# When finished sums are taken out of PSUM: gating traced at each job's end, and fill work kept back behind a chain step

## The chip, the cores and the metric

The kernel runs on one core of one Trainium2 chip. The metric is the device time of one execution in microseconds. Each version is timed in several runs and the median is given. One further execution runs under the hardware profiler, and all durations inside the kernel come from it.

## The reference

One inference step of a hybrid encoder layer for 512 new frames of one stream and 64 frames of a running one, 576 in all, with 2048 channels:

```
h = RMSNorm(x);  z = h @ w_in
y_a = rwkv7(r, k, v, decay, alpha of z) * silu(g_a)
y_b = windowed_attention(q, k, v of z) * silu(g_b)
merged = sigmoid(m_a) * (y_a @ p_a) + sigmoid(m_b) * (y_b @ p_b)
y = RMSNorm(x + merged @ w_o)
```

`rwkv7` carries a 64x64 state per head through time; with 16 heads, each frame updates the state by a decay, a rank-one correction and a new key-value product, and reads it with r. Everything is fp32. The states, the shifted row and the key and value caches are outputs too.

## The kernel before

**Layout.** Channels lie on the 128 partitions and the 576 frames on the free axis. A large product is split in two halves of 256 and 320 frames, one PSUM bank each (`ga`, `gb`). For precision each weight and each input is a pair of a high and a low part, and a product is three matmuls per half (high by high, high by low, low by high).

**Jobs.** A `Job` makes one block of 128 output channels. Its `step()` (line 131) issues the six matmuls of one of its 16 or 8 blocks of input channels. Jobs stand in the list `jobs`, and `pump(n)` issues the next n steps of whichever job is first. `need(job)` (line 158) steps until that job is over and returns its result. When the last step is traced, `done` is called with the two PSUM halves and traces what takes them out: for most jobs `scaled` (line 206), two VectorE products with the RMSNorm factor, which is line 208 in the profile. Weights come in quarters of a job of 16 steps (four steps, `QK`): `prefetch` (line 104) issues the DMA of a quarter (`wr`), ScalarE's copy to its high part (`wh`, line 118) and VectorE's subtraction for the low part (`wl`, line 119), so that up to four quarters are in `ready`. It is called whenever a quarter has been used up, and its work has the planner's high priority.

**Order.** Only TensorE's order is written out by hand: its instructions run in the order in which they are traced. For the other engines a planner chooses the order from dependences and priorities; instructions traced earlier come first where both are ready. Each engine then runs its own queue in order. A block under `tc.issue_after(i)` puts its instructions on i's engine behind i.

**The chain.** The recurrent part handles the heads in eight pairs. In each pair, `rwkv` (line 549) goes through nine chunks of 64 frames in eight steps (the last step has two chunks). A step is a chain: VectorE forms the state `SV` and its scaled form `s0p` (lines 686 to 690), TensorE multiplies them (`p0`, lines 691 and 692), VectorE copies the result to `r0` (line 694), TensorE multiplies by the solved triangle `XT` (line 698), VectorE negates that into `UV` (lines 701 and 702), TensorE forms the next state `sp` and the outputs `py` (lines 707 to 716). While VectorE works, TensorE is filled with steps of jobs: `pump(PUMP["c1"])` behind r0's trace, `pump(PUMP["c2"])` behind UV's, both under `issue_after`, and `pump(PUMP["c3"])` (line 721) behind the outputs, under nothing. Each is one step, with one more in the first c1 of a pair. A job has 16 steps and a pair's chain 25 fills, so a job or a quarter ends now in one kind of fill, now in another.

**The output projections.** Behind the recurrent part come 16 blocks of merged output (lines 793 to 821). For block j there is a job on `p_b` and one on `p_a`, eight steps each, created in the order p_b(j), p_b(j+1), p_a(j), p_a(j+1) for even j. Their `done` returns the PSUM halves as they are. The loop over j takes them out: `gated` (line 793) multiplies the halves with a sigmoid tile `sg` loaded from DRAM (line 801), first `mb` with p_b's result, then `ma` with p_a's; their sum is split into a high and a low part for the last projection. `need` of p_a(j) runs p_b(j+1) and p_a(j), so the gating of p_b(j+1) is traced behind that of p_a(j). Each of the tags `ga` and `gb` has two PSUM buffers.

Of the kernel before, what the change touches and what calls it, by code (L numbers as in the profile page):

```python
# [18 lines left out]
NA = 256  # L19
NB = NT - NA  # L20
# [25 lines left out]
def tile_layer(ctx: ExitStack, tc: tile.TileContext, A: dict):  # L46
# [45 lines left out]
        return hi, lo  # L92

    plan, ready, jobs, spare = deque(), {}, deque(), deque()
    QK = 4

    def halfpass(w, x, out, kk, sl, first, last):
# [6 lines left out]
    def prefetch():  # L104
        while len(ready) < 4 and (plan or spare):
            if not plan:
                spare.popleft()()
                continue
            job, q = plan.popleft()
            with tc.high_priority() if len(h) == KT and jobs[0].own is None else nullcontext():  # L110
                src = wp.tile([P, QK, P], F32, tag="wr", name="wr", bufs=WR)
                nc.sync.dma_start(src.rearrange("p k c -> p (k c)"), job.w[q // 2][:, (q % 2) * QK * P : (q % 2 + 1) * QK * P])
                ready[job, q] = wsplit(src, wp, 4)
# [8 lines left out]
    class Job:  # L122
# [8 lines left out]
        def step(self):  # L131
            k = self.k
            if k == 0 and self.banks:
                self.pa, self.pb = self.banks
            elif k == 0:
                self.pa = pg.tile([P, 512], F32, tag="ga", name="ga")
                self.pb = pg.tile([P, 512], F32, tag="gb", name="gb")
            hi, lo = self.own[k // QK] if self.own else ready[self, k // QK]
            xh, xl = self.xs[k]
            for w, x, f, e in ((hi, xh, k == 0, False), (hi, xl, False, False), (lo, xh, False, k == self.nk - 1)):  # L140
                nc.tensor.matmul(self.pa[:, :NA], w[:, k % QK, :], x[:, 0:NA], start=f, stop=e)  # L141
                nc.tensor.matmul(self.pb[:, :NB], w[:, k % QK, :], x[:, NA:NT], start=f, stop=e)  # L142
            self.k += 1
            if self.k % QK == 0 and not self.own:
                del ready[self, k // QK]
                prefetch()
            if self.k == self.nk:
                jobs.remove(self)
                self.over = True
                self.result = self.done((self.pa[:, :NA], self.pb[:, :NB]))  # L150

    def pump(n):
        for _ in range(n):
# [4 lines left out]
    def need(job):  # L158
        while not job.over:
            jobs[0].step()  # L160
        return job.result

    def mm2(*terms):
# [385 lines left out]
    def rwkv(p, r, k, v, kk, Pd, Qd, b, gate, ahead, before):  # L549
# [48 lines left out]
        for j in range(UB - 1):  # L598
            n, m = UB - 1 - j, j // SP + 1
# [74 lines left out]
        for cs in (*((c,) for c in range(7)), (7, 8)):  # L674
            g = cs[0] // 3
            T, NM, XT, TK = Ts[g], NMs[g], XTs[g], TKs[g]
            at = [(n * L, c, c - 3 * g) for n, c in enumerate(cs)]
            w = len(cs) * L
            if cs[0] == 3 * g:
                py = pst()  # L680
            s0p = r2.tile([P, 2 * L], F32, tag="s0p", name="s0p")
            p0 = pst()
            for n, c, i in at:
                if c not in (0, 8):
                    sp, pt, prev = S_prev
                    dve.scalar_tensor_tensor(SV[E, c, 0:64], sp[E, 0:64], pt[E], prev[E, 0:64], op0=ALU.mult, op1=ALU.add)  # L686
                    dve.scalar_tensor_tensor(SV[O, c, 64:128], sp[O, 0:64], pt[O], prev[O, 0:64], op0=ALU.mult, op1=ALU.add)
                pt = PT[:, c : c + 1]
                dve.tensor_scalar(s0p[E, n : n + L], SV[E, c, 0:64], pt[E], None, op0=ALU.mult)
                dve.tensor_scalar(s0p[O, n : n + L], SV[O, c, 64:128], pt[O], None, op0=ALU.mult)  # L690
                nc.tensor.matmul(p0[E, n : n + L], T[:, i, 0, 0:64], SV[:, c, 0:64], start=True, stop=True)  # L691
                nc.tensor.matmul(p0[O, n : n + L], T[:, i, 1, 0:64], SV[:, c, 64:128], start=True, stop=True)
            r0 = r2.tile([P, 2 * L], F32, tag="r0", name="r0")
            with tc.issue_after(dve.tensor_copy(r0[:, 0:w], p0[:, 0:w]).ins):  # L694
                pump(PUMP["c1"] + (cs[0] == 0) * PUMP["c0"])
            pu = pst()
            for n, c, i in at:
                nc.tensor.matmul(pu[:, n : n + L], XT[:, i, :], r0[:, n : n + L], start=True, stop=True)  # L698
            ui = slice(cs[0], cs[-1] + 1)
            pu3 = pu[:, 0:w].rearrange("p (i c) -> p i c", c=L)  # L700
            dve.tensor_scalar(UV[E, ui, 0:64], pu3[E], -1.0, None, op0=ALU.mult)  # L701
            tip.append(dve.tensor_scalar(UV[O, ui, 64:128], pu3[O], -1.0, None, op0=ALU.mult).ins)
            with tc.issue_after(tip[-1]):
                pump(PUMP["c2"])
            sp = pst()
            for n, c, i in at:
                nc.tensor.matmul(sp[E, n : n + L], TK[:, i, 0:64], UV[:, c, 0:64], start=True, stop=True)  # L707
                nc.tensor.matmul(sp[O, n : n + L], TK[:, i, 64:128], UV[:, c, 64:128], start=True, stop=True)  # L708
            S_prev = (sp, pt, s0p)
            for n, c, i in at:  # L710
                for u, h_ in ((0, E), (1, O)):
                    hc = slice(64 * u, 64 * u + 64)
                    nc.tensor.matmul(py[h_, i * 64 : (i + 1) * 64], SV[:, c, hc], T[:, i, u, 64:128], start=True, stop=False)
                for u, h_ in ((0, E), (1, O)):
                    hc = slice(64 * u, 64 * u + 64)
                    nc.tensor.matmul(py[h_, i * 64 : (i + 1) * 64], UV[:, c, hc], NM[:, i, 128 + 64 * u : 192 + 64 * u], start=False, stop=True)  # L716
                if c >= 7:
                    so = r2.tile([P, L], F32, tag="so", name="so")
                    dve.scalar_tensor_tensor(so, sp[:, n : n + L], PT[:, c : c + 1], s0p[:, n : n + L], op0=ALU.mult, op1=ALU.add)
                    nc.sync.dma_start(A["wkv"][c - 7, p], so)  # L720
            pump(PUMP["c3"])
            if cs[-1] == 3 * g + 2:
                q = slice(g * 192, (g + 1) * 192)
                act(ysb[0][:, q], py[:, 0:192], AF.Copy)  # L724
                yr = r2.tile([P, 192], F32, tag="NU", name="yr", bufs=1)
                act(yr, py[:, 0:192], AF.Copy)  # L726
                pool.tensor_tensor(ysb[1][:, q], yr, ysb[0][:, q].bitcast(F32), op=ALU.subtract)  # L727
# [51 lines left out]
    with ExitStack() as ph:  # L779
        yp = {n: ph.enter_context(tc.tile_pool(name=n, bufs=16)) for n in ("yap", "ybp")}  # L780
        t2 = ph.enter_context(tc.tile_pool(name="t2", bufs=5))
        ys = []
        for n, src in (("ybp", yb_d), ("yap", ya_d)):
            l_ = []
            for k in range(8):
                raw = t2.tile([P, NT], F32, tag="t", name="yraw")
                nc.gpsimd.dma_start(raw, src[k])
                l_.append(split(raw, yp[n], "y", f"y{k}"))
            ys.append(l_)
        while jobs or spare:  # L790
            pump(1)

        def gated(sg, psum, name):
            o = t2.tile([P, NT], F32, tag="t", name=name)
            for (x, y), z in zip(halves(), psum):
                dve.tensor_tensor(o[:, x:y], sg[:, x:y], z, op=ALU.mult)
            return o

        def load_sg(i):
            s = t2.tile([P, NT], F32, tag="sg", name="sg", bufs=6)  # L800
            nc.sync.dma_start(s, sg_d[i])
            return s

        pj = [[None, None] for j in range(KT)]
        for j in range(0, KT, 2):
            for i, n in enumerate(("p_b", "p_a")):
                for d in range(2):
                    pj[j + d][i] = Job([A[n][j + d]], ys[i], lambda psum: psum)
        mg = [None] * KT
        wo = []  # L810
        sg = [[load_sg(2 * j), load_sg(2 * j + 1)] for j in range(2)]
        for j in range(KT):
            if j + 2 < KT:
                sg.append([load_sg(2 * j + 4), load_sg(2 * j + 5)])
            if j == KT - 2:
                wo = [Job(A["w_o"][m], mg, lambda psum: psum) for m in range(KT - DEFER)]
            mb = gated(sg[j][1], need(pj[j][0]), "mb")
            ma = gated(sg[j][0], need(pj[j][1]), "ma")
            dve.tensor_tensor(ma, ma, mb, op=ALU.add)
            mg[j] = split(ma, hp, "hh", f"mg{j}")  # L820

    with ExitStack() as ph:
# [42 lines left out]
        for m in range(KT - DEFER):  # L865
            psum = need(wo[m])
# [123 lines left out]
```

## Time and profile before

| | |
|---|---|
| runs before | 1788.28, 1788.43, 1789.96 us; median 1788.43 us |
| profiled execution | 1788.85 us, of which the span from first to last instruction is 1787.1 us |
| granted TensorE clock, mean over the span | 0.996 |
| HBM traffic | 104 GB/s over the span |

A profile row gives an engine, a source line, the tiles written and read, a count, a time, and often in brackets the idle time of the engine before it and what ended that. "L119 DVE wl" is VectorE's subtraction of line 119. "PE" is TensorE's matmuls, "PEld" its weight loads, ACT is ScalarE, POOL is GpSimd, SP the queue that issues DMAs. In the timeline, rows begin with the start in us from the start of the span and the duration. The chain of work is followed back from the last instruction: each row is a piece of it with its start and length.

### The profile page before, as it was taken

How to read it: one execution, taken by the hardware profiler on the slowest of the kernel's cores; microseconds unless marked ns; L12 is line 12 of the kernel's file. 1: busy time of each engine (PE TensorE's matmuls, PEld its weight loads, DVE VectorE, ACT ScalarE, POOL GpSimd, SP SyncE). 2: the span in 40 equal slices, each digit the busy share in tenths (PEclk: the TensorE clock that was granted, in tenths of full speed). 3: DMA queues.
4: the chain of work that ended last, by engine and by line, in shares of the span. 5: the costliest groups of instructions: out<-in, count | busy, mean ns of one | idle time of the engine just before them, and what ended most of it. 6: DMA issues, size and time to landing. Idle time of an engine off the chain costs nothing.

```text
span 1787.1 us, 36090 instructions
## 1 busy us (share of the span) xinstructions
PE 1752.9 (98%) x14393; PEld 1695.5 (95%) x14393; DVE 1101.6 (62%) x2479; ACT 694.6 (39%) x1308; POOL 336.9 (19%) x448
## 2 busy tenths in 40 slices
PE   9999999999999999999999999999999999999996
PEld 8999999999989999899898998989999999999996
DVE  7445445567777678687786877768655434342224
ACT  7455546543333434244332443424234222243321
POOL 0112212242111312214222241222020000001112
PEclk9999999999999999999999999999999999999998
DMA  7322222333324233233232332323346333253323
GB/s 230 118 87 76 87 87 73 96 96 100 120 82 114 84 98 107 68 113 97 88 110 75 107 95 83 115 72 104 114 137 211 125 123 124 93 168 103 110 73 107
DMA packets 158601, 190.92 MB, mean 107 GB/s; under 512 B 52640, under 2 KB 81600, under 8 KB 158432
## 3 DMA queue, kind: packets, MB, share of 16 engines
q1 hardware_dynamic: 157152, 183.89, 32.9%
q0 software_dynamic: 1280, 4.72, 0.7%
q8 instruction: 113, 1.85, 0.4%
q14 instruction: 56, 0.46, 0.1%
HBM read 158.42 MB, written 27.03 MB: 104 GB/s over the span
## 4 chain that ended last, share of the span: by engine, by line
PE 88%; DVE 7%; DMA 2%; issue 1%; ACT 1%; POOL 1%; DVEq 0%; SPq 0%; ACTq 0%; POOLq 0%
PE gb L142 40%; PE ga L141 34%; DVE wl L119 1%; PE s L707 1%; PE s L691 1%; PE s L698 1%; PE s L142 1%; PE s L168 1%; DVE sg L208 1%; DVE o L861 1%; PE s L141 1%; PE s L305 1%; DVE T L563 1%; DVE T L562 1%; PE s L304 1%
## 5 line engine op out<-in xcount | busy, mean ns | idle before, releaser
L118 ACT ACTIVATE wh<-wr 128x512 fp32r<-128x512 f32 x460 | 288.9, 629 | 719.0 <-PE gb L142 634.4
L119 DVE TENSOR_TENSOR wl<-wr,wh 128x512 fp32r<-128x512 f32 x460 | 333.7, 729 | 267.1 <-ACT wh L118 263.5
L847 POOL TENSOR_TENSOR sq<-sq 128x256 f32<-128x256 f32 (+1 forms) x28 | 25.4, 925 | 378.1 <-ACT sq L841 378.0
L602 DVE TENSOR_TENSOR tmp<-NU,XU 108x84 f32<-108x84 f32 (+23 forms) x248 | 64.2, 259 | 14.3 <-DMA NU<-n_d 8.5
L604 DVE TENSOR_TENSOR XU<-XU,tmp 108x84 f32<-108x84 f32 (+23 forms) x248 | 68.5, 276 | 6.1
L727 POOL TENSOR_TENSOR ylo<-yr,yhi 128x192 fp32r<-128x192 f32 x24 | 14.7, 612 | 298.2 <-ACT yr L726 251.7
L219 POOL COPY praw<-praw 128x7 f32<-128x7 f32 x25 | 9.2, 368 | 218.5 <-DVE praw L216 218.4
L701 DVE TENSOR_SCALAR UV<-s 64x64 f32<-64x64 f32 x64 | 14.4, 224 | 47.6 <-PE s L698 47.6
L329 ACT ACTIVATE sc<-sc,nm 128x256 f32<-128x256 f32 (+2 forms) x80 | 37.1, 466 | 13.6 <-DVE nm L327 13.5
L384 ACT ACTIVATE sg<-sg 128x576 f32<-128x576 f32 x32 | 21.9, 684 | 49.1 <-DVE sg L208 49.0
L235 POOL TENSOR_TENSOR gateb<-gateb,z 128x576 f32<-128x576 f32 x8 | 11.4, 1420 | 150.3 <-ACT gateb L234 150.3
L334 POOL TENSOR_TENSOR sc<-sc,es 128x768 f32<-128x768 f32 x16 | 27.6, 1723 | 63.7 <-ACT wh L118 58.0
L565 POOL TENSOR_TENSOR BK<-k,Qd 64x192 f32<-64x192 f32 x48 | 34.0, 707 | 27.0 <-DVE k L544 21.3
L222 POOL TENSOR_TENSOR d<-praw 128x576 f32<-128x576 f32 x25 | 35.5, 1421 | 0.0
L564 POOL TENSOR_TENSOR BK<-b,Qd 64x192 f32<-64x192 f32 x48 | 32.6, 680 | 11.3 <-PE s L583 8.4
L686 DVE SCALAR_TENSOR_TENSOR SV<-s,PT,s0p 64x64 f32<-64x64 f32 x56 | 15.4, 276 | 27.4 <-PE s L708 27.0
L223 DVE SCALAR_TENSOR_TENSOR d<-d,vec,praw 128x576 f32<-128x576 f32 x25 | 22.2, 890 | 15.8 <-POOL d L222 15.8
L742 DVE RECIPROCAL sd<-sd 128x576 f32<-128x576 f32 x8 | 30.0, 3753 | 3.1 <-ACT sd L741 3.0
L540 DVE RECIPROCAL nrm<-nrm 128x576 f32<-128x576 f32 x8 | 30.0, 3750 | 1.1 <-ACT nrm L539 1.1
L698 PEld LDWEIGHTS s<-r,XT 128*128 128x128 f32 x144 | 22.9, 190 | 6.7 <-DVE r L694 6.7
L698 PE MATMUL s<-r,XT 128*128 128x64 f32 x144 | 23.8, 256 | 4.8 <-DVE r L694 4.8
L724 ACT ACTIVATE yhi<-s 128x192 fp32r<-128x192 f32 x24 | 8.0, 332 | 52.5 <-PE s L716 51.9
(1147 smaller groups left out, 7248.9 us busy)
## 6 DMA issues: line engine op xcount, KB each, us to landing
wr<-in_w_in SPq DMA_DIRECT2D x340, 256.0 KB
wr<-in_w_o SPq DMA_DIRECT2D x56, 256.0 KB
sg_d<-sg SPq DMA_DIRECT2D x32, 288.0 KB
sg<-sg_d SPq DMA_DIRECT2D x32, 288.0 KB
wr<-in_p_b SPq DMA_DIRECT2D x32, 256.0 KB
wr<-in_p_a SPq DMA_DIRECT2D x32, 256.0 KB
x<-in_xT SPq DMA_DIRECT2D x16, 288.0 KB
n_d<-nm SPq DMA_DIRECT2D x24, 192.0 KB
```

The source lines that it names most:

```text
L118: act(hi, src, AF.Copy)
L119: dve.tensor_tensor(lo, src, hi.bitcast(F32), op=ALU.subtract)
L141: nc.tensor.matmul(self.pa[:, :NA], w[:, k % QK, :], x[:, 0:NA], start=f, stop=e)
L142: nc.tensor.matmul(self.pb[:, :NB], w[:, k % QK, :], x[:, NA:NT], start=f, stop=e)
L222: pool.tensor_tensor(d, p[:, :, 0:64], p[:, :, 1:65], op=ALU.subtract)
L329: act(sc[:, a:b], sc[:, a:b], AF.Exp, bias=nm[:, i : i + 1], accum_out=dn[:, i : i + 1])
L540: dve.reciprocal(nrm, nrm)
L564: pool.tensor_tensor(BK[h_, :, 64 * u : 64 * u + 64], b[h_, cs_, :], Qd[h_, cs_, :], op=ALU.mult)
L565: pool.tensor_tensor(BK[h_, :, 64 - 64 * u : 128 - 64 * u], k[h_, cs_, :], Qd[h_, cs_, :], op=ALU.mult)
L602: dve.tensor_tensor(t_, NU[:, j, j + 1 : UB].unsqueeze(1).to_broadcast([SP * UN, m, n]), XU[:, 0:m, j : j + 1].to_broadcast([SP * UN, m, n ...
L604: dve.tensor_tensor(XU[:, 0:m, j + 1 : UB], XU[:, 0:m, j + 1 : UB], t_, op=ALU.add)
L698: nc.tensor.matmul(pu[:, n : n + L], XT[:, i, :], r0[:, n : n + L], start=True, stop=True)
```

## The change

A function `later(f)` runs f at once, or puts it in a queue while the list `holding` is not empty; `flush()` runs what is queued. `step` hands `prefetch` and the job's `done` (now in a method `end`) to `later`. `holding` is filled only around the c3 fill of a chain step. The queue is run behind the next chain step's r0 copy, inside its `issue_after`; at the end of `need`; where a weight quarter is wanted that isn't loaded yet; and at once behind the last chain step. So the scaled copies and the weight quarter that a c3 fill triggers are traced one half step later. TensorE's order stays as it was.

In the output projections, `done` of each job now does the gating itself, so that `mb` and `ma` are traced at the end of the job that they belong to.

```
+    held, holding = deque(), []
+
+    def later(f):
+        if holding:
+            held.append(f)
+        else:
+            f()
+
+    def flush():
+        while held:
+            held.popleft()()
...
+            if not self.own and (self, k // QK) not in ready:
+                flush()
...
                 del ready[self, k // QK]
-                prefetch()
+                later(prefetch)
             if self.k == self.nk:
                 jobs.remove(self)
                 self.over = True
-                self.result = self.done((self.pa[:, :NA], self.pb[:, :NB]))
+                later(self.end)
+
+        def end(self):
+            self.result = self.done((self.pa[:, :NA], self.pb[:, :NB]))
...
         while not job.over:
             jobs[0].step()
+        flush()
         return job.result
...
             with tc.issue_after(dve.tensor_copy(r0[:, 0:w], p0[:, 0:w]).ins):
+                flush()
                 pump(PUMP["c1"] + (cs[0] == 0) * PUMP["c0"])
...
+            holding.append(cs)
             pump(PUMP["c3"])
+            holding.pop()
+            if cs[-1] == 8:
+                flush()
...
-                    pj[j + d][i] = Job([A[n][j + d]], ys[i], lambda psum: psum)
+                    pj[j + d][i] = Job([A[n][j + d]], ys[i], lambda psum, i=i, j=j + d: gated(sg[j][1 - i], psum, "ma" if i else "mb"))
...
-            mb = gated(sg[j][1], need(pj[j][0]), "mb")
-            ma = gated(sg[j][0], need(pj[j][1]), "ma")
+            mb, ma = [need(i) for i in pj[j]]
```

## The prediction

> **What bounds the kernel now.** I read the page's first part, then the waits of PE, then the chain of work that ended last, and then single stretches of the timeline.
>
> ```profile
> span 1787.1 us, 36090 instructions
> PE 1752.9 (98%) x14393; PEld 1695.5 (95%) x14393; DVE 1101.6 (62%) x2479; ACT 694.6 (39%) x1308; POOL 336.9 (19%) x448
> ```
>
> TensorE is busy for 98% of the span, so the kernel is bound by PE nearly everywhere, and a change that adds and removes no instruction can only win what PE spends waiting: the span less PE's busy time, 1787.1 - 1752.9 = 34.2 us, at most. The waits of PE (engine, line, releaser; then total us, times, longest) begin with the two that matter here:
>
> ```profile
> PE s L698 <- DVE r L694: 4.8, 7, 0.7
> PE ga L141 <- ACT wh L118: 4.1, 9, 0.5
> ```
>
> The first belongs to the chain step (L694 is the copy r0, L698 the product behind it), seven times. The second is in the output projections. Both totals are too small a measure of the loss, because matmuls that start late also run at half pace for a moment; so I measure the loss as time between like points.
>
> **Part one, the gating.** Four jobs make a pair: p_b(j), p_b(j+1), p_a(j), p_a(j+1). The windows view, cut at the job ends, shows where a pair loses time (columns: stretch, its length, PE, PEld, DVE, ACT, POOL busy, clock, DMA share, GB/s). The chain of work has the same stall at the first and at the last of eight pairs:
>
> ```profile
> 1371.20:1378.60 7.40, 6.94 (x51) 6.60 (x50) 4.27 (x8) 1.99 (x4) 0.00 (x0) 1.00 0.49 154
> 1378.60:1385.00 6.40, 6.40 (x50) 6.40 (x50) 3.54 (x6) 1.95 (x4) 0.00 (x0) 1.00 0.39 125
> 1385.00:1391.40 6.40, 6.40 (x50) 6.40 (x50) 2.11 (x4) 1.26 (x3) 0.00 (x0) 1.00 0.40 133
> 1391.40:1397.80 6.40, 6.40 (x49) 6.30 (x48) 1.39 (x2) 1.31 (x3) 0.00 (x0) 1.00 0.25 81
> ...
> 1371.19 0.64 ACT wh L118
> ...
> 1556.77 0.64 ACT wh L118
> ```
>
> Three jobs take 6.40 us with PE full; the one that begins at 1371.2, p_a(j+1), takes longer. The stalls lie (1556.77 - 1371.19) / 7 = 26.51 us apart, four full jobs would be 25.60 us, so a pair loses 0.91 us. What does p_a(j+1) wait for? PE's timeline in that place:
>
> ```profile
> 1371.11 0.31 PE L142 MATMUL gb<-y7h,wl 128*128 128x320 f32 x1
> 1371.88 0.35 PE L141 MATMUL ga<-y0h,wh 128*128 128x256 f32 x1 [0.46 <-ACT wh L118]
> 1372.18 0.41 PE L142 MATMUL gb<-y0h,wh 128*128 128x320 f32 x1
> ```
>
> and DVE's in the same place:
>
> ```profile
> 1371.31 0.42 DVE L796 TENSOR_TENSOR ma<-sg,ga 128x256 f32<-128x256 f32 x1 [1.96 <-PE ga L141]
> 1371.65 0.48 DVE L796 TENSOR_TENSOR ma<-sg,gb 128x320 f32<-128x320 f32 x1
> 1373.32 0.41 DVE L796 TENSOR_TENSOR mb<-sg,ga 128x256 f32<-128x256 f32 x1
> ```
>
> The profile names ACT's weight copy, but that copy fills the slot which the job just ended gave back; it is for a quarter three quarters ahead. The PSUM times fit better: the copy of bank ga ends at 1371.73 and PE writes ga at 1371.88; the copy of gb ends at 1372.13 and PE writes gb at 1372.18. So p_a(j+1) takes the banks that p_a(j) has only just filled, while the result of p_b(j+1), finished one job earlier at about 1364.8, lies unread until the mb copy at 1373.32, because its gating is traced after p_a(j)'s. The change traces that gating at its job's end. Then p_b(j+1)'s banks are free some 5 us before p_a(j+1) begins, and p_a(j)'s some 5 us before the next p_b. The same copies run, in another order; in the 6.40 us stretches DVE has at least 2.8 us free (6.40 - 3.54), which hides them. If that cover were gone, each pair of copies would cost the 0.82 us from 1371.31 to 1372.13. Nothing is late next: a job of 6.40 us uses two weight quarters, and three are in stock, 9.6 us. Gain 8 x 0.91 = **7.3 us**. Bounds: nothing, if the wait really is the weight copy, and 7.3 us.
>
> [...]
>
> **Part two, the chain.** Each of the eight head pairs runs eight chain steps: L691, a fill (c1), L698, a fill (c2), L707 and what follows, a fill (c3). Only what a c3 fill triggers is kept back, to behind the next step's r0 copy. Rows of the chain of work in one head pair:
>
> ```profile
> 723.52 0.20 PE s L691
> ...
> 728.09 0.20 PE s L691
> ...
> 731.84 0.26 PE s L691 x2
> ...
> 735.77 0.20 PE s L691
> ...
> 736.13 0.82 DVE sg L208 x2
> 736.95 0.60 DVE wl L119
> 737.55 0.15 DVE r L694
> 737.74 0.43 PE s L698 x2
> ...
> 740.52 0.20 PE s L691
> ...
> 744.28 0.20 PE s L691
> ```
>
> A step without trouble takes 3.75 us (728.09 to 731.84). The one from 735.77 takes 4.75 us: a job and a weight quarter ended in the c3 fill ahead of it, and the two scaled copies (0.82) and wl (0.60) stand on DVE ahead of r0. That loses 1.00 us. It is not all given back: the kept-back work now stands between r0 and UV (L701). This order exists in the trace, where a job ends in a c1 fill (the last head pair). DVE's timeline, first r0 of an untroubled step, then that place:
>
> ```profile
> 728.42 0.23 DVE L694 COPY r<-s 128x64 f32<-128x64 f32 x1 [0.25 <-PE s L692]
> ...
> 1306.29 0.23 DVE L694 COPY r<-s 128x64 f32<-128x64 f32 x1
> 1306.55 0.42 DVE L208 TENSOR_TENSOR sg<-rstd,ga 128x256 f32<-128x256 f32 x1
> ...
> 1307.29 0.69 DVE L119 TENSOR_TENSOR wl<-wr,wh 128x512 fp32r<-128x512 f32 x1
> 1307.89 0.21 DVE L701 TENSOR_SCALAR UV<-s 64x64 f32<-64x64 f32 x1
> ```
>
> The next L691 in the chain of work, and ACT's weight copy ahead of the stalled step:
>
> ```profile
> 1309.96 0.20 PE s L691
> ...
> 735.54 0.63 ACT L118 ACTIVATE wh<-wr 128x512 fp32r<-128x512 f32 x1 [0.16 <-PE gb L142]
> ```
>
> r0 follows L691 by 0.33 us (728.42 - 728.09), so r0 would start at 735.77 + 0.33 = 736.10, and 736.13 is when DVE comes free. With both copies and wl behind it, UV comes 1307.89 - 1306.29 = 1.60 us later, at 737.73; from UV to the next L691 it is 1309.96 - 1307.89 = 2.07 us, so 739.80. The step is then 4.03 us: 0.28 us stay, **0.72 us** go. wh is done at 736.17, before wl is due, so wl does not wait. Queued behind the kept-back work are UV and the next SV on DVE, and on PE L707; that is what the 0.28 us are. The weight quarter itself moves by under 1 us and is due after three more quarters; on SP the weight DMA moves with it by as much, and the sg store some 0.3 us; on ACT the sigmoid moves by as much; POOL gets nothing. All of them are far from due.
>
> How often? In the chain of work the same two rows stand once in each of six head pairs (the first and the last of them below), and the last head pair has them at its second step, from another count of fills:
>
> ```profile
> 622.75 0.82 DVE sg L208 x2
> ...
> 1189.87 0.82 DVE sg L208 x2
> ...
> 1281.20 0.20 PE s L691
> ...
> 1286.14 0.48 DVE sg L208
> ...
> 1290.19 0.20 PE s L691
> ```
>
> Six (from 622.75 to 1189.87, and 736.13 - 622.75 = 113.4 us from one to the next) times 0.72 is 4.3 us. In the last head pair two steps take 1290.19 - 1281.20 = 8.99 us against 731.84 - 723.52 = 8.32. Its second step starts at 1281.20 + 4.57 = 1285.77; with r0 at 1286.10, UV at 1287.70 and L691 at 1289.77, 0.42 us go. Together **4.7 us**. Upper bound: if wl and the copies land behind UV, all of it goes, 6 x 1.00 + 0.67 = 6.7 us. Lower bound 0: the work merely moves in front of UV and costs there what it cost in front of r0. I take 4.7, for the row at 1306.29 is this very order. The other c3 fills end only a quarter, without a job; in a step of 3.75 us UV is due 3.75 - 2.07 = 1.68 us behind L691 and r0 is done at 0.33 + 0.23 = 0.56, so a wl of 0.69 fits between them. They are set at nothing, with PE's own fill as the cover, and cost at most their 0.69 us each if it is gone.
>
> **Sum.** 7.3 + 4.7 = 12.0 us. The profiled execution took 1788.85 us, so 1776.85 us; the median of the timed runs is 0.42 lower (1788.43), so about **1776.5 us**.
>
> **Rivals.**
> 1. Gating works, the chain gives nothing: the kept-back copies delay UV as much as they delayed r0. For it: wl and both copies come to 1.42 us in either place. Against it: the 1306.29 row, and that in an untroubled step 1.1 us lie between r0 and UV, which take most of the 1.42 us. 1788.43 - 7.3 = 1781.1 us.
> 2. The pair bubble stays: the wait of p_a(j+1) is for weights, as the profile's releaser says, or two banks per half are too few in any order; or the planner, which orders every engine but PE, still puts the copy behind p_a(j)'s, so that this half of the change doesn't do what it says. For it: the releaser's name. Against it: the times of the gb bank. 1788.43 - 4.7 = 1783.7 us. If also the chain gives nothing, 1788.4.
> 3. Slower: the gating copy of p_b(j+1), now early in DVE's queue, waits for its sigmoid tile, and every wl behind it waits too, until PE runs out of weights. The tile's load is issued by SP here:
>
> ```profile
> 1372.16 0.33 SPq L801 DMA_DIRECT2D sg<-sg_d  x1
> 1374.16 0.33 SPq L801 DMA_DIRECT2D sg<-sg_d  x1
> ```
>
> The copy that needs them would start at about 1391.4, over 17 us later. It decides only where a load takes longer than that plus the 9.6 us of weights in stock, some 27 us; to end above 1792 us, PE would have to lose 2 us in each of eight pairs: 1788.4 - 12.0 + 8 x 2 = 1792.4 us. With a DMA share of 0.25 to 0.49 in those stretches I see nothing that would hold a load so long.
>
> **How the numbers follow.** Both parts: 0.74. Gating alone: 0.11. Chain alone: 0.08. Neither: 0.03. Slower: 0.04. The likeliest case spans 1788.43 - 7.3 - 6.7 = 1774.4 to 1781.1 us with the chain's bounds, which takes in the first rival; with 0.8 us, half the spread of the three runs before, on either side: 1773.6 to 1781.9 us. What is left outside is 0.15. A measurement of this kernel can tell about 0.2%, 3.6 us, from no change: the first two cases and the chain alone (4.7 us less) are beyond that, so faster 0.93, same 0.03, slower 0.04.
>
> **What would show it.** Right: in the waits of PE, L698 <- DVE r falls from seven entries to none or nearly, and L707 <- DVE UV gains about seven small ones; the windows of the output projections come out at 6.40 us each, 25.6 us a pair; the mb copies of odd j start within 0.3 us of their job's end. Wrong: a pair of 26.5 us (second rival), steps of 4.7 us at the same places (first), or DVE idle for DMA sg ahead of an L796 copy (third). What would make it wrong beyond these is a planner that reorders DVE or ACT elsewhere, in the preparation of the next head pair, because the tracing order has moved.

## The result, and the profile after

| | before | changed |
|---|---|---|
| median of six runs each | 1788.53 us (1788.28 to 1789.96) | 1777.88 us (1776.92 to 1778.52) |
| ratio, 95% interval | | 0.9938 [0.9925, 0.9951] |
| span of the profiled execution | 1787.1 us | 1776.8 us |

The change makes the kernel 10.65 us faster; 12.0 us were forecast. The profiled execution of the changed kernel is the slowest of its six. The changed kernel was run again later, on another chip: 1777.37 us against 1789.40 us there, 12.03 us less (ratio 0.9932 [0.9919, 0.9944]).

The page of the changed kernel, first part. Lines are shifted: the fill's products are L155 and L156, wl is L131, r0 is L712, UV is L720 and L721, the first product of a chain step is L709, the one behind r0 is L717, the one behind UV is L726.

```profile
span 1776.8 us, 36081 instructions
PE 1750.5 (99%) x14393; PEld 1696.1 (95%) x14393; DVE 1101.7 (62%) x2479; ACT 694.4 (39%) x1308; POOL 337.2 (19%) x448
```

No engine has a matmul, copy or product more or less. What went is mostly waiting: the span less PE's busy time is 26.3 us, where it was 34.2. PE's busy time itself is 2.4 us less. The waits of PE and of its weight loads (PEld) in the changed kernel that answer to those shown before, then, in a fence of its own, the waits for UV in the kernel before:

```profile
PE ga L155 <- ACT wh L130: 1.6, 2, 1.1
PE s L726 <- DVE UV L720: 0.8, 2, 0.5
...
PEld s L726 <- DVE UV L720: 2.5, 9, 0.7
```

```profile
PE s L707 <- DVE UV L701: 0.7, 2, 0.5
...
PEld s L707 <- DVE UV L701: 1.2, 2, 0.7
```

The wait of the product behind r0, seven times and 4.8 us before, is gone from PE's list. In its place the weight load that needs UV waits seven times more, nine for two, and these waits are short: 2.5 us in all for 1.2. On PE itself the wait for UV is as it was. The nine waits of ga have become two, and these two are others, as is seen below.

**The output projections.** The windows view of the changed kernel, cut at four job ends (length, PE, PEld, DVE, ACT, POOL, clock, DMA share, GB/s), then its timeline of PE and, in fences of their own, of DVE and of ACT:

```profile
1361.10:1367.50 6.40, 6.40 (x50) 6.40 (x49) 2.20 (x4) 1.33 (x3) 0.00 (x0) 1.00 0.43 145
1367.50:1373.90 6.40, 6.40 (x50) 6.40 (x49) 3.54 (x6) 1.90 (x4) 0.00 (x0) 1.00 0.40 128
1373.90:1380.30 6.40, 6.40 (x50) 6.40 (x49) 3.54 (x6) 1.95 (x4) 0.00 (x0) 1.00 0.41 129
1380.30:1386.70 6.40, 6.40 (x50) 6.40 (x49) 2.12 (x4) 1.26 (x3) 0.00 (x0) 1.00 0.42 127
```

```profile
1367.36 0.31 PE L156 MATMUL gb<-y7h,wl 128*128 128x320 f32 x1
1367.50 0.28 PE L155 MATMUL ga<-y0h,wh 128*128 128x256 f32 x1
```

```profile
1361.16 0.42 DVE L819 TENSOR_TENSOR mb<-sg,ga 128x256 f32<-128x256 f32 x1 [1.91 <-PE ga L155]
...
1367.56 0.42 DVE L819 TENSOR_TENSOR ma<-sg,ga 128x256 f32<-128x256 f32 x1 [1.96 <-PE ga L155]
```

```profile
1367.43 0.63 ACT L130 ACTIVATE wh<-wr 128x512 fp32r<-128x512 f32 x1 [2.57 <-PE gb L156]
```

All four jobs take 6.40 us, and PE goes from p_a(j) to p_a(j+1) without a gap at 1367.50. The mb copy of p_b(j+1) now starts 0.06 us behind its job's end (1361.10) and not behind p_a(j)'s copies, so its bank has been free for over 5 us when p_a(j+1) wants one. ScalarE's weight copy, which the profile of the kernel before names as the releaser in this place, still starts at the end of p_a(j), at 1367.43, and lasts until 1368.06. PE begins p_a(j+1) at 1367.50, in the middle of it, so this job does not need that copy.

**The chain.** The same step as before, in the chain of work and in DVE's timeline of the changed kernel:

```profile
734.83 0.20 PE s L709
...
736.08 0.17 PE s L717 x2
...
737.09 0.29 PE s L726 x2
...
738.86 0.20 PE s L709
...
742.62 0.20 PE s L709
```

```profile
735.19 0.23 DVE L712 COPY r<-s 128x64 f32<-128x64 f32 x1
735.45 0.42 DVE L226 TENSOR_TENSOR sg<-rstd,ga 128x256 f32<-128x256 f32 x1
735.79 0.68 DVE L131 TENSOR_TENSOR wl<-wr,wh 128x512 fp32r<-128x512 f32 x1
736.39 0.48 DVE L226 TENSOR_TENSOR sg<-rstd,gb 128x320 f32<-128x320 f32 x1
736.78 0.21 DVE L720 TENSOR_SCALAR UV<-s 64x64 f32<-64x64 f32 x1
```

The step takes 738.86 - 734.83 = 4.03 us. From r0 to UV it is 1.59 us, because the three kept-back instructions stand between them.

**Where the time went.** The span cut at four points: the first product of the first and of the last chain step, the start of p_b(1), the start of the first job on w_o. Each row is the difference of their starts.

| stretch | before | changed | difference |
|---|---|---|---|
| up to the first chain step | 488.43 | 488.20 | -0.23 |
| first to last chain step | 821.46 | 816.90 | -4.56 |
| last chain step to p_b(1), "the passage" | 48.57 | 49.60 | +1.03 |
| p_b(1) to the first job on w_o | 205.69 | 198.40 | -7.29 |
| first job on w_o to the end | 222.93 | 223.66 | +0.73 |
| span | 1787.08 | 1776.76 | -10.32 |

So both terms of the forecast are there in nearly full size, and 1.8 us come back in two stretches for which the forecast had no term. The experiments ask first whether the two halves are what they seem, and then what these two stretches are.

### The profile page after: what moved, and what is told of

It is laid out like the page before. It is cut to its first block, busy times and chain, and to the rows that moved or that the text cites. A ratio compares the mean times of both kernels' runs of the same rounds, so it can differ in the third digit from the quotient of the medians.

```text
span 1776.8 us, 36081 instructions
## 1 busy us (share of the span) xinstructions
PE 1750.5 (99%) x14393; PEld 1696.1 (95%) x14393; DVE 1101.7 (62%) x2479; ACT 694.4 (39%) x1308; POOL 337.2 (19%) x448
## 4 chain that ended last, share of the span: by engine, by line
PE 89%; DVE 6%; issue 2%; DMA 2%; POOL 1%; ACT 1%; DVEq 0%; SPq 0%; ACTq 0%; POOLq 0%
PE gb L156 41%; PE ga L155 35%; PE s L726 1%; PE s L709 1%; DVE wl L131 1%; PE s L156 1%; PE s L186 1%; PE s L717 1%; DVE o L883 1%; PE s L155 1%; PE s L323 1%; DVE T L581 1%; DVE T L580 1%; PE s L322 1%; DVE tmp L620 1%
## 5 line engine op out<-in xcount | busy, mean ns | idle before, releaser
L131 DVE TENSOR_TENSOR wl<-wr,wh 128x512 fp32r<-128x512 f32 x460 | 333.7, 729 | 238.6 <-ACT wh L130 234.9
L720 DVE TENSOR_SCALAR UV<-s 64x64 f32<-64x64 f32 x64 | 14.3, 224 | 43.9 <-PE s L717 43.9
L712 DVE COPY r<-s 128x64 f32<-128x64 f32 x64 | 14.9, 233 | 20.5 <-PE s L710 19.7
L91 POOL TENSOR_TENSOR rkl<-rk,rkh 128x576 fp32r<-128x576 f32 x8 | 11.5, 1441 | 84.3 <-ACT rkh L90 72.0
```

The costliest lines, as they stand in the source:

```text
L131: dve.tensor_tensor(lo, src, hi.bitcast(F32), op=ALU.subtract)
```

## The experiments

**One half at a time.** The first run leaves the c3 fill as it was, the second the gating.

```
-            holding.append(cs)
             pump(PUMP["c3"])
-            holding.pop()
```

> Only the gating is traced at each job's end; the c3 fill keeps nothing back. If a bank held too long was the wait, the four jobs of a pair take 25.6 us instead of 26.5, and the time falls by 8 x 0.91 = 7.3 us to about 1781.2 us; the chain steps stay at 4.75 us. If the passage between the recurrent part and the output projections swallows part of what the chain wins, nothing is swallowed here, for nothing was won ahead of it. If the wait was for weights, pairs stay at 26.5 us and the time at 1788.5 us.

```
-  Job([A[n][j + d]], ys[i], lambda psum, i=i, j=j + d: gated(sg[j][1 - i], psum, ...))
+  Job([A[n][j + d]], ys[i], lambda psum: psum)
...
-            mb, ma = [need(i) for i in pj[j]]
+            mb = gated(sg[j][1], need(pj[j][0]), "mb")
+            ma = gated(sg[j][0], need(pj[j][1]), "ma")
```

> Only the c3 fill's work is kept back; the gating is traced as before. Steps of 4.75 us become 4.03 us in six head pairs and the last pair wins 0.42, so the chain ends 4.7 us earlier; pairs stay at 26.5 us. If the passage to the output projections is bound by the chain, the time is 1788.5 - 4.7 = 1783.8 us. If it is bound by transfers that start no earlier or run no faster, about 1 us of it is lost there and the time is about 1785 us.

Gating alone: 1781.73 us against 1789.12 us before on that chip, 7.4 us less (ratio 0.9958 [0.9946, 0.9971]); a pair takes 25.60 us and the steps 4.75 us. Keeping back alone: 1784.85 us, 4.3 us less (0.9975 [0.9966, 0.9984]); steps of 4.03 to 4.06 us, a pair still 26.51 us. The halves add up to 11.7 us, which lies between the 10.65 and the 12.03 us of the whole change, so nothing here shows that they depend on one another. The passage took 48.70 us in the first and 48.53 us in the second: it swallows nothing of what the chain wins. So the about 1785 us for the second came out by the number and not for the reason given there. Its chain is 817.92 us long, 1.0 us longer than the changed kernel's, nearly all of it in the first two steps of two head pairs. DVE's timeline of that run at one of them, then POOL's:

```profile
1176.70 1.55 DVE L131 TENSOR_TENSOR wl<-wr,wh 128x512 fp32r<-128x512 f32 x1
1178.28 0.28 DVE L704 SCALAR_TENSOR_TENSOR SV<-s,PT,s0p 64x64 f32<-64x64 f32 x1
```

```profile
1176.28 1.42 POOL L253 TENSOR_TENSOR gatea<-gatea,z 128x576 f32<-128x576 f32 x1
```

wl usually takes 0.69 us. Here it began while a product ran on POOL, and ended 0.55 us behind that product's end (1176.28 + 1.42 = 1177.70), as if it had waited for it; the step in which it lies and the one behind it were 0.19 and 0.35 us longer (4.75 against 4.56 and 4.10 against 3.75). In the changed kernel the same product ended at 1175.63, 0.55 us ahead of the same wl, which took 0.69 us. No run here takes the POOL product away, so that it caused the delay is my reading of the two rows. All twelve profiles agree with it by the order of the two: 322 of their 5520 subtractions wl began while a two-input instruction on POOL had more than 0.3 us left, and every one of them took over 0.72 us; the 602 that began ahead of the POOL instruction which they overlap took no longer than that.

**The order of the jobs, in place of the order of the gating.** If the stall was a bank held too long, it must go as well if the kernel before runs its jobs in the order in which its loop gates them.

```
         for j in range(0, KT, 2):
-            for i, n in enumerate(("p_b", "p_a")):
-                for d in range(2):
+            for d in range(2):
+                for i, n in enumerate(("p_b", "p_a")):
```

> The kernel before with nothing changed but the order of the output projections' jobs: p_b(j), p_a(j), p_b(j+1), p_a(j+1), so that each result is gated as soon as its job is over without any change of the gating code. By the theory of the bank that is held too long the pair's stall goes here too (25.6 us for four jobs, about 1781 us), unless the start pays for y_a being needed one job earlier. If two banks per half are too few in any order, or weights are late, four jobs stay at 26.5 us and the time at 1788.5 us.

1781.58 us, 7.5 us less (0.9959 [0.9947, 0.9972]); four jobs take 25.60 us. DVE's timeline of this run:

```profile
1364.65 0.42 DVE L796 TENSOR_TENSOR ma<-sg,ga 128x256 f32<-128x256 f32 x1 [1.91 <-PE ga L141]
...
1371.05 0.42 DVE L796 TENSOR_TENSOR mb<-sg,ga 128x256 f32<-128x256 f32 x1 [1.91 <-PE ga L141]
```

Each copy now follows its own job, 6.40 us apart, with the old gating code. The number of banks is as before, the weights are loaded by the same code, and the stall is gone. So the wait was for the bank, as the row of ACT at 1367.43 says too, and the weight copy that the profile names as its releaser only happened to end last there.

**The rest of a chain step.** If the 0.28 us that stay in a step are the sum of three instructions in a gap of 1.1 us, they go when the gap gets one item at a time. The first try releases one item at each r0:

```
-                flush()
+                if held:
+                    held.popleft()()
```

> The changed kernel, but behind each r0 copy only one kept-back item is traced: the weight quarter (0.69 us on VectorE) behind the next r0, the scaled copies (0.82 us) behind the one after it. By my account 1.1 us are free between r0 and UV, so each fits and the 0.28 us left per step go: 4.03 becomes 3.75 us six times and the last pair wins 0.25 more, 1777.9 - 1.9 = 1776.0 us. If the 0.28 us come from something else than the sum of 1.42 us on VectorE, steps stay at 4.03 us and the time at 1777.9 us.

It did not come out faster than the changed kernel: 1779.39 us, 9.7 us below the kernel before on that chip (0.9944 [0.9931, 0.9958]), where the changed kernel was 10.65 and 12.03 us below it. The step in question is 3.75 us, as expected, but the next one is 4.25 us. DVE's timeline of that next step:

```profile
739.08 0.22 DVE L712 COPY r<-s 128x64 f32<-128x64 f32 x1 [0.32 <-PE s L710]
739.34 0.42 DVE L226 TENSOR_TENSOR sg<-rstd,ga 128x256 f32<-128x256 f32 x1
739.68 0.48 DVE L226 TENSOR_TENSOR sg<-rstd,gb 128x320 f32<-128x320 f32 x1
740.20 0.22 DVE L721 TENSOR_SCALAR UV<-s 64x64 f32<-64x64 f32 x1
740.43 0.69 DVE L131 TENSOR_TENSOR wl<-wr,wh 128x512 fp32r<-128x512 f32 x1
741.16 0.23 DVE L722 TENSOR_SCALAR UV<-s 64x64 f32<-64x64 f32 x1
```

The scaled copies fit, as counted: UV comes 1.12 us behind r0. But this step's own c1 fill ends a weight quarter, and the planner has put its wl between the two halves of UV. My account left that item out. The second try skips such a step:

```
-                if held:
+                if held and jobs[0].k % QK != QK - 1:
```

> The changed kernel, with one kept-back item per r0 and none behind an r0 whose own c1 fill ends a weight quarter. By the account of VectorE's free 1.1 us between r0 and UV, both the weight quarter and the scaled copies now stand alone where they stand, steps of 4.03 and 4.25 us become 3.75 us, and the chain wins 6 x 0.28 + 0.25 = 1.9 us on the changed kernel. If a kept-back item costs PE something by itself, steps with one stay above 3.75 us and the time stays within 1 us of the changed kernel.

1775.51 us, in the same set in which the changed kernel had 1777.37 us; ratio to the kernel before 0.9921 [0.9908, 0.9935]. Steps of 4.03 and 4.25 us are 3.75 us now. The chain is 815.58 us long, 1.6 us shorter than that of the changed kernel in the same set (817.14); 1.9 were expected, and against them stands the last step of each of six pairs, 4.05 to 4.07 us in place of 3.93, for which no cause was looked for.

The account then says what more there is: steps of 3.93 us, where a c2 fill's wl falls between the halves of SV, and steps of 4.56 us, where a job ends in c1.

```
-    def later(f):
-        if holding:
+    def later(f, kind):
+        if kind in holding:
...
+                holding.append("end")
                 pump(PUMP["c1"] + (cs[0] == 0) * PUMP["c0"])
+                holding.clear()
...
             with tc.issue_after(tip[-1]):
+                holding.extend(("load", "end"))
                 pump(PUMP["c2"])
+                holding.clear()
```

Here `later` takes a second argument, "load" for a weight quarter and "end" for a finished job, and holds only what is named. The c3 fill names both, as the c2 fill does.

> As the run with skipped steps, and the c2 fill keeps its weight quarter and its finished job back too, the c1 fill its finished job. By the same account the steps of 3.93 us (a wl between the halves of SV) become 3.75 us and those of 4.56 us where a job ends in c1 become 3.75 us: some 13 x 0.18 + 0.35 + 2 x 0.81 = 4.3 us on top of 1.9, so about 6 us below the changed kernel. If weights come too late because they are asked for later, PE waits for wh or wl appear in the chain and eat it.

1772.24 us, 5.1 us below the changed kernel, and a ratio of 0.9905 [0.9892, 0.9919] to the kernel before. Its chain of work and DVE's timeline at the place shown all along:

```profile
724.81 0.20 PE s L709
...
728.56 0.20 PE s L709
...
732.32 0.20 PE s L709
```

```profile
732.69 0.22 DVE L712 COPY r<-s 128x64 f32<-128x64 f32 x1
732.94 0.69 DVE L131 TENSOR_TENSOR wl<-wr,wh 128x512 fp32r<-128x512 f32 x1
733.78 0.22 DVE L723 TENSOR_SCALAR UV<-s 64x64 f32<-64x64 f32 x1
...
740.17 0.23 DVE L712 COPY r<-s 128x64 f32<-128x64 f32 x1 [0.24 <-PE s L710]
740.43 0.42 DVE L226 TENSOR_TENSOR sg<-rstd,ga 128x256 f32<-128x256 f32 x1
740.77 0.48 DVE L226 TENSOR_TENSOR sg<-rstd,gb 128x320 f32<-128x320 f32 x1
741.29 0.22 DVE L723 TENSOR_SCALAR UV<-s 64x64 f32<-64x64 f32 x1
```

All steps but the first and the last of a pair are 3.75 to 3.76 us now: 728.56 - 724.81 and 732.32 - 728.56 here. The first, which has one fill more, stays at 4.56 us. The weight quarter and the scaled copies each have a gap of their own, UV 1.09 and 1.12 us behind r0. The chain is 811.72 us long, 5.4 us shorter than the changed kernel's, of 6.2 expected; the last step of a pair, 3.96 to 3.98 us, is where some of the rest lies. PE's waits show no new one for weights in the chain.

**The two stretches without a term.** Two runs of the same set carry this, with the profiles of the others. The changed kernel again:

> The changed kernel once more, on the chip of the three others of this set. Steps of 4.03 us and pairs of 25.6 us come again; the time is 10 to 11 us below the kernel before. If the last sum over partitions runs at a granted clock of 0.5 or 1.0 by where the clock's own period falls, that product takes 1.2 or 0.7 us here as it may; if it is fixed by the change, it takes 1.2 us again.

Steps of 4.04 to 4.06 us, pairs of 25.60 us, and 12.03 us below the kernel before, more than the 10 to 11 that were expected. The passage took 49.05 us this time. Over twelve profiles of ten kernels it lies between 48.53 and 49.60 us, and neither half of the change moves it. The excess of the changed kernel there, in the waits of PE's weight loads between the last chain step and p_b(1), before and then changed:

```profile
PEld ga L141 <- ACT wh L118: 0.6, 1, 0.6
```

```profile
PEld ga L155 <- ACT wh L130: 2.1, 2, 1.3
```

There wh stands in ACT's queue between the splits of y, which wait for y's loads from DRAM, and those landed at different times in the two executions: ScalarE waited 1.83 us for the load of one part of y_b in the first profile of the changed kernel, and 0.91 us for the same part in the second. What sets it was not tried.

Behind the last projection, most of the excess is the clock. In the changed kernel and, in the fence behind, in the kernel before, the last sum over partitions; first PE's timeline, then the windows view of that product (the clock stands third from the end):

```profile
1762.39 1.22 PE L877 MATMUL s<-sq,ones 128*128 128x256 f32 x2 [2.96 <-ACT sq L863]
```

```profile
1762.40:1763.60 1.20, 1.20 (x2) 0.48 (x2) 0.00 (x0) 0.33 (x1) 0.00 (x0) 0.50 1.04 358
```

```profile
1773.43 0.70 PE L855 MATMUL s<-sq,ones 128*128 128x256 f32 x2 [2.97 <-ACT sq L841]
```

```profile
1773.40:1774.20 0.80, 0.70 (x2) 0.30 (x2) 0.00 (x0) 0.41 (x2) 0.00 (x0) 0.97 1.05 360
```

The product and the wait ahead of it are the same; at a granted clock of 0.50 it takes 1.22 us. In the kernel before it takes 0.70 us, at a clock of 0.97 over a window that reaches a little past its end. To see whether the idle time does it, PE was given something to do in it, products whose result nobody reads:

```
             nc.tensor.matmul(s[:, :n], ones, acc[hv], start=True, stop=False)
+            if hv == 0:
+                idle = pst()
+                for _ in range(20):
+                    nc.tensor.matmul(idle[:, :NA], mg[0][0][:, 0:P], mg[0][0][:, 0:NA], start=True, stop=True)
```

> The changed kernel with 20 products of 256 columns whose result nobody reads, in TensorE's wait of 2.96 us ahead of the last sum over partitions. If that sum runs at a granted clock of 0.50 because TensorE idled ahead of it, it runs at 1.00 now and takes 0.6 to 0.7 us instead of 1.22, and the time falls by 0.5 us or, averaged over the runs in which the clock held anyway, less. If the clock has another cause, the sum takes 1.22 us as before.

1776.85 us, beside 1777.37 of the changed kernel in the set: 0.5 us less by the medians, though the two sets of runs overlap (1776.48 to 1777.25 and 1776.69 to 1778.38). The trace of this run:

```profile
1758.12 2.74 PE L880 MATMUL s<-mg0h 128*128 128x256 f32 x20
1761.45 0.70 PE L881 MATMUL s<-sq,ones 128*128 128x256 f32 x2 [0.58 <-ACT sq L863]
```

The wait is 0.58 us and the product 0.70 us, at a clock of 1.00. That is not yet a proof: in ten profiles with the wait of 2.97 us the clock fell ahead of the product in five and not in the other five.

The traces show where the two fives differ. Cut finely, the windows view gives the moment at which the clock falls; in the profile of the changed kernel it is 1761.61 us:

```profile
1761.40:1761.60 0.20, 0.00 (x0) 0.00 (x0) 0.20 (x2) 0.00 (x0) 0.00 (x0) 1.00 1.02 320
1761.70:1761.90 0.20, 0.00 (x0) 0.00 (x0) 0.18 (x1) 0.00 (x0) 0.00 (x0) 0.50 1.08 390
```

By the record of the granted clock in each trace, it is full from a few us behind the span's start (6.04 us in the kernel before, 7.16 us in the changed one) and falls once. The time between is 1751.04 to 1768.10 us, and in each of the twelve profiles it is a whole number, 513 to 518, of periods of 3.413 us; in the kernel before it is 1768.10 us and in the changed one 1754.45 us, four periods less. So in these profiles the clock fell only at moments 3.413 us apart, and where these lay in the kernel differed from execution to execution. In the five profiles in which the clock fell, such a moment lay 2.11 to 2.84 us behind the start of the wait; in the five in which it held, 0.27 to 1.23 us, and there it fell at the next moment, behind the product.

In the two profiles with the unread products (this one and the next set's) the moment lay at 0.29 and 0.94 us, where the clock held without them too. So neither profile shows that the products saved the 0.52 us. What both show is the moment after, at 3.70 and 4.35 us: without the products the clock fell there, at 3.68 to 4.64 us in the five profiles, and with them it fell one period later still. That it was the idle TensorE that lowered the clock here, and the unread work that held it, is how I read these twelve profiles. That the products win the 0.52 us in an execution whose moment lies late in the wait is an expectation from that reading, and no profile here shows it.

**The best of both.** Last, the kernel that keeps back the work of all fills, with the warm tail and, beside it, once more without:

> The kernel that keeps back the work of all fills, with the 20 unread products of the warm tail. If the two gains are independent, the time is 0.5 us below that kernel where its last sum ran at a clock of 0.50: about 1771.7 us, and some 17.5 us below the kernel before. If they are not, no less than 1772.2 us.

> The kernel that keeps back the work of all fills once more, on the same chip as the run with the warm tail: 17 us below the kernel before, give or take the 1 us by which the passage from the recurrent part to the output projections differs from run to run.

1771.46 us with the warm tail, 1771.82 us without, against 1789.09 us before on that chip (0.9904 [0.9887, 0.9920] and 0.9905 [0.9890, 0.9920]). The kernel without it had its last product at 0.70 us this time, the same program that had it at 1.22 us in the set before, so in that profile there was nothing to win. Whether the warm tail wins anything on top in the median can't be told from these runs. Both beat the kernel before by over 17 us. In the one set that holds both, the kernel that keeps back all fills is 5.1 us below the changed kernel.

## Why the prediction was right, and by how much it was off

The forecast was 1776.5 us, the result 1777.88 us, within the range, and its steps can be gone through one by one.

- **The bound.** "At most 34.2 us", the waits of PE, is not a strict bound: 2.4 of the 10.3 us came out of PE's busy time, by the slow starts behind a wait that the same paragraph of the prediction speaks of. In the kernel before, the product on gb at 1372.18, behind the wait of 0.46 us, is followed by the next one after 0.26 us, where 0.14 to 0.15 is usual, at a granted clock of 1.00; of the 0.91 us that a pair lost, the wait was 0.46.
- **The gating, 7.3 us.** 7.29 us in the profile, 7.4 us in the run that has nothing else. The reading of the stall as a held bank and not a late weight, against the releaser that the profile names, is shown by the run with another job order, and by the weight copy that ends behind the start of p_a(j+1) in the changed kernel.
- **The chain, 4.7 us.** The step of 4.03 us came out six times (4.03 to 4.04), and so did the 0.42 us of the last pair (4.43 to 4.01). It was taken from one place in the trace where the new order already existed, and this is why. The chain's total is 4.56 us: the steps win the forecast sum, and 0.19 us come back between the last step of the seventh pair and the first of the eighth (75.67 us in place of 75.48). That is not chance: this stretch takes 75.60 to 75.72 us in the six profiles that keep back the c3 fill's work alone, and 75.41 to 75.48 in the other six. What costs it was not followed up. That the 0.28 us left over come from a gap of 1.1 us that holds one item and not two is shown by the runs that release one at a time. The order of the three kept-back instructions (wl between the two scaled copies) was not foreseen and costs nothing.
- **Edits set at nothing.** Other c3 fills: their steps are 3.75 us before and after. The weight quarter's delay: no new wait for weights in the chain. Both held.
- **The sum.** The medians fall 1.35 us short of the forecast 12.0, the two profiles 1.7. What is missing between the profiles is not in a term but in two that were left out: 1.03 us in the passage and 0.73 us behind the last projection, 0.52 of them (1.22 - 0.70) the clock. Both differ between executions of one program, so how near the total came is in part luck: the profile before had the clock at full at the end, the profile after had it at half. On the later chip the medians differ by 12.03 us, as forecast; the kernel before was not profiled there, so that number can't be taken apart.
- **The rivals.** The chain gave nothing: it gave 4.56 us. The bubble stays: it went. A copy waiting for its sigmoid tile: no such wait stands in the trace. Two banks per half too few in any order: they were enough once they were given back in time, 25.60 us a pair.

## What to carry to other kernels

When an engine with a hand-written order waits for a buffer, ask which instruction gives that buffer back and where that instruction stands in its own queue: a result that lies finished and unread can hold up a job that has nothing to do with it. Work moved off one point of a chain goes to another, so count the free time between the new neighbours and put one item into each gap, with the items that belong there already counted in. The best price for a new order is a place in the old trace where it already occurs.

## What the runs showed of the hardware

- In twelve profiles the granted clock fell only at moments 3.413 us apart (513 to 518 whole periods at full clock). In a wait of 2.97 us on TensorE it fell to 0.50 where such a moment lay 2.11 to 2.84 us into the wait, in five of ten profiles, among them one and not the other of two profiles of the same program; it held where the moment lay 0.27 to 1.23 us into it. Between 1.23 and 2.11 us no run shows anything. The windows view of the changed kernel over that wait:

```profile
1758.90:1762.30 3.40, 0.52 (x3) 0.12 (x2) 2.98 (x5) 0.38 (x2) 0.00 (x0) 0.90 0.89 306
```

  A mean clock of 0.90 is 0.50 for a fifth of the 3.4 us, so the clock fell about 0.7 us before the wait was over, as the moment of 1761.61 us says too.
- In the run that keeps back the c3 fill's work alone, wl took 1.55 us in place of 0.69 when a product on POOL had begun 0.42 us before it, and in all twelve profiles it took over 0.72 us whenever a two-input instruction on POOL, begun earlier, had more than 0.3 us left.
- In the kernel before, the releaser that the profile names for the wait at 1371.88 ended 0.09 us later than the true one (wh at 1371.82, the copy of ga at 1371.73).
